# Every second weight block's low part made by an accumulating GpSimd transfer in a float32 decoder layer

## The chip, the core and the metric

The kernel runs on one core of one Trainium2 chip. The metric is the device time of one execution, in microseconds (us). The engines are named as the profile names them: PE is TensorE's matmuls and PEld its weight loads, DVE is VectorE, ACT is ScalarE, POOL is GpSimd and SP is SyncE, which here only issues loads. L92 is line 92 of the kernel's file. "q" behind an engine's name is its instruction queue.

## The reference

One decoder layer on 256 tokens of width 2048, all in float32: a gated feed-forward half, a mixer of two groups of attention heads, and a second feed-forward half, each behind an RMS norm.

```python
def swiglu(x, w_gate, w_up, w_down):
    return (jax.nn.silu(x @ w_gate) * (x @ w_up)) @ w_down

h = h + 0.5 * swiglu(rms_norm(h, norm_ffn1_g), ffn1_w_gate, ffn1_w_up, ffn1_w_down)
u = rms_norm(h, norm_mix_g)
q_f, k_f, v_f, f_logit, q_s, k_s, v_s = jnp.split(u @ w_in, SPLIT_POINTS, axis=-1)
...
o = jnp.concatenate([rms_norm(o_fox, out_norm_fox_g), rms_norm(o_swa, out_norm_swa_g)], axis=-1)
h = h + o @ w_out
h = h + 0.5 * swiglu(rms_norm(h, norm_ffn2_g), ffn2_w_gate, ffn2_w_up, ffn2_w_down)
```

The feed-forward width is 5632, so each of its three weights has 2048 x 5632 elements. The attention stands on 16 forgetting heads and 16 window heads (4 key-value heads) of width 64.

## The kernel before, in words

The weights are read once, in blocks of 128 partitions x 1024 float32 (512 KB). A matmul of type float32r takes operands with short mantissas, so each block is cut in two parts that add up to it: `whi`, the block rounded to float32r, and `wlo`, what the rounding left. The activations are cut in the same way. A product is then three products of parts: high by high, high by low, low by high.

`weights` (L89 to L95) does this for one block: SP issues the load into `raw` (L92), ScalarE makes `whi` by a rounding copy (L93), and VectorE makes `wlo` as `raw` minus `whi` (L94). The tiles come from `weight_tiles` (L83), which has four buffers each of `raw`, `whi` and `wlo`. A buffer is given to a later block when all readers of the earlier one are done: for `raw` these are L93 and L94, for `whi` and `wlo` the matmuls.

Two functions use the blocks. `columns` (L207) serves the feed-forward halves and the output projection: a block holds four row tiles of 128 x 256 weights, and `column_major` (L197) takes from it eight pairs of matmuls, L202 with `whi` against both parts of the activations (512 columns), L203 with `wlo` against their high part (256 columns). In a feed-forward half, `gate_up` (L243) loops over 22 chunks of 256 columns, four blocks of gate and four of up each; `gated` (L229) evacuates and combines them. `down` (L251) loops over 8 chunks of 11 blocks each. `token_major` (L277) serves the mixer's input projections, with two row tiles a block and the weights as the moving operand. In the output projection GpSimd multiplies (L681) and adds (L682) the evacuated tiles; it also adds up squares (L163).

The order of the instructions on each engine is set by the tile framework's scheduler from its own estimates of time; `weights` is called under a high priority, so loads, roundings and subtractions are placed as early as buffers allow. In the trace there are 648 roundings and as many subtractions: 600 of 128x1024, 32 of 128x776 (the window heads' projection) and 16 of 128x512, which are the first pieces of the first chunk. Those first pieces call `weights` with tiles of their own.

Of the kernel before, what the change touches and what calls it, by code (L numbers as in the profile page):

```python
# [17 lines left out]
P = 128  # L18
# [16 lines left out]

# columns of the constants and of the packed vectors
C_ID, C_ONE, C_TRI, C_MSK, C_INVF = 0, 128, 256, 384, 896
# [31 lines left out]
def hybrid_layer(ctx: ExitStack, tc: tile.TileContext, a: dict, out: bass.AP):  # L69
# [11 lines left out]

    # ---------------------------------------------------------------- weights
    def weight_tiles():  # L83
        raw = wp.tile([P, 1024], F32, tag="raw", name="raw", bufs=4)
        hi = wp.tile([P, 1024], F32R, tag="whi", name="whi", bufs=4)
        lo = wp.tile([P, 1024], F32R, tag="wlo", name="wlo", bufs=4)
        return raw, hi, lo

    def weights(src, tiles=None, at=0):  # L89
        """A block of weights: loaded, and cut into two parts of 12 bits that add up to it."""  # L90
        raw, hi, lo = (t[:, at : at + src.shape[1]] for t in tiles or weight_tiles())
        nc.sync.dma_start(raw, src)  # L92
        nc.scalar.copy(hi, raw)  # L93
        nc.vector.tensor_tensor(out=lo, in0=raw, in1=hi.bitcast(F32), op=ALU.subtract)  # L94
        return hi, lo  # L95

    # -------------------------------------------------------------- constants
    cst = keep.tile([P, C_END], F32, name="cst")
# [14 lines left out]
    def new_u():  # L113
        """The two parts of 2048 x 256 activations, by tiles of 128 rows."""
        halves = [half_u(0), half_u(1)]
        return lambda k: halves[k // 8][:, k % 8]
# [3 lines left out]

    # ----------------------------------------------------------- small helpers
    def mean_rsqrt(pool, ssq, n, width, tag):
        """1 / sqrt(ssq / width + EPS) for [P, n] sums, by Newton's steps."""
        x = pool.tile([P, n], F32, tag=tag + "x", name=tag + "x")
        y = pool.tile([P, n], F32, tag=tag + "y", name=tag + "y")
        t = pool.tile([P, n], F32, tag=tag + "t", name=tag + "t")
        nc.vector.tensor_scalar(
            out=x, in0=ssq, scalar1=1.0 / width, scalar2=EPS, op0=ALU.mult, op1=ALU.add
        )
        nc.vector.tensor_scalar(  # L130
            out=t.bitcast(I32), in0=x.bitcast(I32), scalar1=1, scalar2=None,
            op0=ALU.logical_shift_right,
        )
        nc.vector.tensor_scalar(
            out=y.bitcast(I32), in0=t.bitcast(I32), scalar1=-1.0, scalar2=float(0x5F3759DF),
            op0=ALU.mult, op1=ALU.add,
        )
        for _ in range(3):
            nc.vector.tensor_tensor(out=t, in0=y, in1=y, op=ALU.mult)
            nc.vector.scalar_tensor_tensor(  # L140
                out=t, in0=t, scalar=-0.5, in1=x, op0=ALU.mult, op1=ALU.mult
            )
            nc.vector.scalar_tensor_tensor(
                out=y, in0=t, scalar=1.5, in1=y, op0=ALU.add, op1=ALU.mult
            )
        return y

    def split_scaled(dst, src, gain):
        """dst = the two parts of src * gain, gain one value a partition."""
        nc.scalar.mul(dst[:, 0, :], src, gain)  # L150
        nc.vector.scalar_tensor_tensor(  # L151
            out=dst[:, 1, :], in0=src, scalar=gain, in1=dst[:, 0, :].bitcast(F32),
            op0=ALU.mult, op1=ALU.subtract,
        )

    def add_squares(ssq, src, first):
        """ssq [P, 2, SEQ] (+)= src squared."""
        if first:
            nc.scalar.activation(ssq, src, AF.Square)
            return  # L160
        sq = sp.tile([P, 2, SEQ], F32, tag="sqh", name="sqh", bufs=2)
        nc.scalar.activation(sq, src, AF.Square)  # L162
        nc.gpsimd.tensor_tensor(out=ssq, in0=ssq, in1=sq, op=ALU.add)  # L163

    def rstd_tokens(ssq, width, tag):
        """[P, NT], the tokens' 1 / rms, from sums of squares by partition."""
        pb = small_ps()
# [8 lines left out]
    def rstd_rows(ssq, width, tag):  # L176
        """[P, SEQ], the same in every partition."""
        r = rstd_tokens(ssq, width, tag + "t")
# [13 lines left out]

    # ------------------------------------------------------- feed-forward half
    def banks(acc):
        return acc[:, 0, :], acc[:, 1, :]

    def column_major(acc, w, u, k0, k, last, cols=(0, 1)):  # L197
        """acc[j] += (128 x 256 weights).T @ parts of u; its halves' sum is the product."""
        hi, lo = w
# [7 lines left out]
    def columns(acc, src, nk, u, apart=0):  # L207
        """acc = the products of nk row tiles; the columns' halves one after the other in the last ones."""
        late = []
# [57 lines left out]
    def into(u, ssq, gcol):  # L267
        """Of two row tiles of h that are finished: the parts for u, and the squares."""

# [7 lines left out]
    def token_major(acc, u, nk, src_w, width=512):  # L277
        """acc[:, t, :width] = u.T @ weights, for both token tiles."""
        for kg in range(nk // 2):
# [11 lines left out]

    # ------------------------------------------------------------ first FFN
    sp = ctx.enter_context(tc.tile_pool(name="sp", bufs=1))
    u1 = new_u()
    ss1 = sp.tile([P, 2, SEQ], F32, tag="ss", name="ss1")
    with tc.tile_pool(name="f1", bufs=1) as fp:
        hT = fp.tile([P, KF, 2, SEQ], F32R, name="hT1")
        # the tensor engine's clock rises while it works: products of zeros until the first operands come
        zero = fp.tile([P, 512], BF16, name="zero")
# [33 lines left out]

    # ------------------------------------------------------------ token mixer
    with tc.tile_pool(name="mix", bufs=1) as mp:
        ap_ = mp

        # angles of the rotation, reduced to [-pi, pi]
        n2 = NT * 32
# [62 lines left out]

        # ---- attention of four heads at a time
        def softmax_pv(scores, mask, vals, dst, nsk=None):
            """scores(j, blk, out): S of head j; vals(kb, j): values of key block kb; dst gets the heads' rows."""
            s0 = ap_.tile([P, 4, P], F32, tag="s0", name="s0", bufs=2)
# [36 lines left out]
            for i, s in ((0, s0), (1, s1_)):  # L443
                for j in range(4):
                    nc.vector.tensor_scalar_mul(s[:, j, :], s[:, j, :], rd[:, i, j : j + 1])
            # probabilities by key: of the first keys for all queries, of the second for the second
            p0 = ap_.tile([P, 4, SEQ], F32, tag="p0", name="p0", bufs=1)
# [15 lines left out]

        # ---- window heads and forget gates: columns f | q | k | v
        prs = ap_.tile([P, NT, NSW], F32, tag="prs", name="prs")
# [5 lines left out]

        # log of the forget gates, and its running sum
        z = ap_.tile([P, NT, NH], F32, name="z")
# [15 lines left out]

        # norms of the heads of q and k, and the rotation  # L490
        nqk = NH + NKV
# [16 lines left out]

        # of two k heads: the q heads, in pairs, and the k heads with zeros in the other half
        qk = [unit_tile([P, 6, SEQ], F32, "qk%d" % aa) for aa in range(2)]  # L510
        for aa in range(2):
            nc.gpsimd.memset(qk[aa][:, 4:6, :], 0.0)
        for t in range(NT):
# [3 lines left out]
            for j0, nj, tb in ((0, NH, tq), (NH, NKV, tk)):  # L517
# [3 lines left out]
                for es_, xa, ta, xb, tb_, op in (  # L521
# [7 lines left out]
                    nc.vector.tensor_tensor(out=o_, in0=o_, in1=w_, op=op)  # L529
            # q: pairs of heads of neighbouring k heads; k: each head with zeros in the other half  # L530
            rb_ = rw[:, t, :].unsqueeze(2).broadcast_to([P, nqk, HD])
# [37 lines left out]

        # ---- forgetting heads, by half: q and k carry the running sums  # L570
        ofx = ap_.tile([P, 8, SEQ], F32, name="ofx")
# [3 lines left out]
        def fox_qk(hf):  # L575
            aug[hf] = [unit_tile([HD + 2, 2, 4, SEQ], F32, "aug%d" % jj) for jj in range(2)]
            for i in range(2):
# [16 lines left out]
                for t in range(NT):  # L594
                    # columns 64 and 65: c and -1 for q; 1 and c for k
                    qa = ap_.tile([P, 8, HD + 2], F32, tag="qp", name="qa", bufs=2)
# [72 lines left out]

        # ---- output projection: window half, then forgetting half  # L670
        u2 = new_u()
# [13 lines left out]

    # ------------------------------------------------------------ second FFN
    rb2 = rstd_rows(ss2, D, "rb")
# [6 lines left out]

# ---- the arrays as the program reads them: blocks of weights as they are used, and vectors packed
def _arrays(x, positions, norm_ffn1_g, ffn1_w_gate, ffn1_w_up, ffn1_w_down, norm_mix_g, w_in, b_forget,
# [5 lines left out]
    def blocks(w, rows, cols):  # L702
        """By column block and group of row tiles, [P, tiles * columns] blocks."""
        n, m = w.shape
        w = w.reshape(n // P // rows, rows, P, m // cols, cols).transpose(3, 0, 2, 1, 4)
        return w.reshape(m // cols, n // P // rows, P, rows * cols)
# [57 lines left out]
```

## Time and profile before

| | |
|---|---|
| median of 2 runs | 1857.54 us (1857.29 to 1857.79) |
| the profiled execution's span, first to last instruction | 1855.6 us, 1.9 us below that median |
| TensorE, matmuls | 1842.8 us busy, 99% of the span |
| VectorE | 1142.0 us, 62% |
| ScalarE | 895.5 us, 48% |
| GpSimd | 91.1 us, 5% |
| DMA | 337.99 MB, 182 GB/s mean; the load queue holds the 16 engines 57.4% of the span |
| granted TensorE clock | 1.000 |

The profile is of one execution. Its own time is not listed apart from its span; what lies around the span is taken as the 1.9 us between the span and the median. Matmuls are pipelined and overlap, so a sum of their durations is more than the time that they take together. A row of a group of instructions has the line, the engine, the operation, what it writes and reads, the count, then the busy time and the mean of one in ns, and then the idle time of the engine before them with what ended it. A row of the list of waits reads: engine, tile and line that waited, what it waited for, us in total, times, the longest in us. A row of a timeline begins with start and duration in us. DMA issues give KB each and the us from issue to landing.

### The profile page before, as it was taken

To read this page: it belongs to the slowest core of one execution; us is meant where nothing else is said; L and a number is where in the kernel's file an instruction comes from. 1 tells how busy PE (TensorE), PEld (TensorE's weight loads), DVE (VectorE), ACT (ScalarE), POOL (GpSimd) and SP (SyncE) were. 2 spreads that over 40 slices of the span, in tenths; PEclk is the share of its full clock that TensorE was granted. 3 is DMA by queue.
4 is the path that set the end of the run, shared out by engine and by line. 5 is a ranking of instruction groups with operands and counts; after the bars stand their busy time and mean duration, and the time that the engine had idled before them with its cause. 6 is when DMAs were issued, how large, how long until landed. Compare 5 with 4: busy or idle time off the path is not lost.

```text
span 1855.6 us, 26310 instructions
## 1 busy us (share of the span) xinstructions
PE 1842.8 (99%) x10428; PEld 1604.5 (86%) x10428; DVE 1142.0 (62%) x1394; ACT 895.5 (48%) x1182; POOL 91.1 (5%) x73
## 2 busy tenths in 40 slices
PE   8999999999999999999999999999999999999999
PEld 6888888888888888998888888888888888888887
DVE  8556665655655555658767797566666666544443
ACT  6444444444444444455766655444444444443432
POOL 2000000000000000000001462000000000000000
PEclk9999999999999999999999999999999999999999
DMA  7666555665555565565345356666665655666663
GB/s 254 190 188 187 184 190 183 187 187 184 191 184 191 185 189 185 170 203 173 115 147 159 114 161 188 188 191 193 190 186 192 193 187 190 192 189 202 191 200 114
DMA packets 97211, 337.99 MB, mean 182 GB/s; under 512 B 10816, under 2 KB 12992, under 8 KB 97088
## 3 DMA queue, kind: packets, MB, share of 16 engines
q1 hardware_dynamic: 94752, 334.10, 57.4%
q10 hardware_dynamic: 2336, 2.21, 0.3%
q8 instruction: 82, 1.34, 0.3%
q14 instruction: 41, 0.34, 0.0%
HBM read 334.17 MB, written 2.10 MB: 181 GB/s over the span
## 4 chain that ended last, share of the span: by engine, by line
PE 97%; DVE 2%; issue 1%; ACT 1%; DMA 0%; DVEq 0%
PE acc L202 53%; PE acc L203 28%; PE acc L189 4%; PE acc L191 4%; PE acc L190 4%; DVE wlo L94 1%; PE sm L202 1%; PE sm L203 1%; PE sc L558 1%; PE sm L454 1%; PE sm L460 1%; PE sc L630 1%; DVE u L151 0%; PE sm L609 0%; PE sm L461 0%
## 5 line engine op out<-in xcount | busy, mean ns | idle before, releaser
L94 DVE TENSOR_TENSOR wlo<-raw,whi 128x1024 fp32r<-128x1024 f32 (+2 forms) x648 | 794.8, 1229 | 667.8 <-ACT whi L93 667.5
L93 ACT CAST whi<-raw 128x1024 fp32r<-128x1024 f32 (+2 forms) x648 | 665.7, 1029 | 897.0 <-PE acc L202 629.6
L202 PE MATMUL acc<-u,whi 128*128 128x512 f32 x2944 | 1033.2, 395 | 1.7 <-DVE t L226 1.0
L203 PE MATMUL acc<-u,wlo 128*128 128x256 f32 x2944 | 826.9, 281 | 4.2 <-DVE wlo L94 4.2
L202 PEld LDWEIGHTS acc<-u,whi 128*128 128x128 f32 x2944 | 551.9, 188 | 132.1 <-DVE t L226 1.3
L203 PEld LDWEIGHTS acc<-u,wlo 128*128 128x128 f32 x2944 | 556.2, 189 | 7.8 <-DVE wlo L94 7.0
L202 PE MATMUL acc<-hT,whi 128*128 128x512 f32 x1320 | 463.5, 393 | 0.0
L203 PE MATMUL acc<-hT,wlo 128*128 128x256 f32 x1320 | 373.3, 283 | 0.0
L202 PEld LDWEIGHTS acc<-hT,whi 128*128 128x128 f32 x1320 | 247.9, 188 | 57.3
L203 PEld LDWEIGHTS acc<-hT,wlo 128*128 128x128 f32 x1320 | 248.2, 188 | 0.0
L189 PE MATMUL acc<-whi,u 128*128 128x512 f32 (+1 forms) x320 | 120.1, 375 | 0.6 <-ACT pr L583 0.6
L191 PE MATMUL acc<-whi,u 128*128 128x512 f32 (+1 forms) x320 | 119.4, 373 | 0.0
L190 PE MATMUL acc<-wlo,u 128*128 128x512 f32 (+1 forms) x320 | 119.4, 373 | 0.0
L226 DVE TENSOR_TENSOR t<-acc,t 128x512 f32<-128x512 f32 x119 | 81.2, 682 | 0.0
L225 ACT COPY t<-acc 128x512 f32<-128x512 f32 x119 | 68.9, 579 | 0.7 <-PE acc L203 0.7
L189 PEld LDWEIGHTS acc<-whi,u 128*128 128x128 f32 x320 | 60.1, 188 | 8.6 <-ACT pr L583 0.8
L191 PEld LDWEIGHTS acc<-whi,u 128*128 128x128 f32 x320 | 60.1, 188 | 7.9 <-issue 0.6
L190 PEld LDWEIGHTS acc<-wlo,u 128*128 128x128 f32 x320 | 60.2, 188 | 7.1
L234 DVE TENSOR_TENSOR t<-t,rb 128x512 f32<-128x512 f32 x88 | 60.7, 692 | 2.9
L202 PE MATMUL acc<-oTf,whi 128*128 128x512 f32 x128 | 45.4, 396 | 1.0 <-DVE t L226 1.0
L163 POOL TENSOR_TENSOR ssm<-ssm,sqh 128x512 f32<-128x512 f32 x7 | 9.6, 1367 | 704.8 <-ACT sqh L162 704.8
L151 DVE SCALAR_TENSOR_TENSOR u<-h,vec,u 128x256 fp32r<-128x256 f32 x48 | 40.1, 875 | 3.7 <-ACT u L150 3.7
(185 smaller groups left out, 812.6 us busy)
## 6 DMA issues: line engine op xcount, KB each, us to landing
raw<-in_wd SPq DMA_DIRECT2D x176, 512.0 KB, 3.5
raw<-in_wg SPq DMA_DIRECT2D x172, 512.0 KB, 3.5
raw<-in_wu SPq DMA_DIRECT2D x172, 512.0 KB, 3.5
raw<-in_wf SPq DMA_DIRECT2D x48, 512.0 KB, 3.9
raw<-in_wo SPq DMA_DIRECT2D x32, 512.0 KB, 3.6
raw<-in_ws SPq DMA_DIRECT2D x32, 388.0 KB, 3.1
h<-in_xT SPq DMA_DIRECT2D x8, 256.0 KB, 5.1
raw<-in_wg SPq DMA_DIRECT2D x8, 256.0 KB, 4.4
```

The lines of the kernel that those rows point to most:

```text
L93: nc.scalar.copy(hi, raw)
L94: nc.vector.tensor_tensor(out=lo, in0=raw, in1=hi.bitcast(F32), op=ALU.subtract)
L151: nc.vector.scalar_tensor_tensor(out=dst[:, 1, :], in0=src, scalar=gain, in1=dst[:, 0, :].bitcast(F32), op0=ALU.mult, op1=ALU.subtract,)
L189: nc.tensor.matmul(o, lhsT=shi, rhs=mhi, start=start, stop=False)
L190: nc.tensor.matmul(o, lhsT=shi, rhs=mlo, start=False, stop=False)
L191: nc.tensor.matmul(o, lhsT=slo, rhs=mhi, start=False, stop=stop)
L202: nc.tensor.matmul(acc[j], lhsT=hi[:, s], rhs=u(k), start=(k == 0), stop=False)
L203: nc.tensor.matmul(acc[j][:, 0:SEQ], lhsT=lo[:, s], rhs=u(k)[:, 0, :], start=False, stop=(k == last - 1))
L225: nc.scalar.copy(t, acc[:, :, SEQ:])
L226: nc.vector.tensor_tensor(out=t, in0=acc[:, :, 0:SEQ], in1=t, op=ALU.add)
L234: nc.vector.tensor_tensor(out=v[nm], in0=v[nm], in1=rbb, op=ALU.mult)
L454: nc.tensor.transpose(bt[:, j * P : (j + 1) * P], src[:, j, :], ident)
```

## The change

Of the blocks that get their own tiles, the second, fourth and so on make `wlo` in another way. ScalarE writes minus `raw`, rounded to float32r, into `wlo`; then GpSimd issues a transfer from `raw` to `wlo` that adds to what is there. The sum is again `raw` minus its rounded part. `raw` has three buffers where it had four, and `wlo` five where it had four. The other blocks, and the first chunk's pieces, are made as before. Below, "odd" blocks are those with the subtraction and "even" ones those with the transfer.

```diff
     def weight_tiles():
-        raw = wp.tile([P, 1024], F32, tag="raw", name="raw", bufs=4)
+        raw = wp.tile([P, 1024], F32, tag="raw", name="raw", bufs=3)
         hi = wp.tile([P, 1024], F32R, tag="whi", name="whi", bufs=4)
-        lo = wp.tile([P, 1024], F32R, tag="wlo", name="wlo", bufs=4)
+        lo = wp.tile([P, 1024], F32R, tag="wlo", name="wlo", bufs=5)
         return raw, hi, lo

+    turn = [0]
+
     def weights(src, tiles=None, at=0):
         raw, hi, lo = (t[:, at : at + src.shape[1]] for t in tiles or weight_tiles())
         nc.sync.dma_start(raw, src)
         nc.scalar.copy(hi, raw)
-        nc.vector.tensor_tensor(out=lo, in0=raw, in1=hi.bitcast(F32), op=ALU.subtract)
+        turn[0] += tiles is None
+        if tiles is None and turn[0] % 2 == 0:
+            nc.scalar.mul(lo, raw, -1.0)
+            nc.gpsimd.dma_start(lo, raw, accum_op=ALU.add)
+        else:
+            nc.vector.tensor_tensor(out=lo, in0=raw, in1=hi.bitcast(F32), op=ALU.subtract)
         return hi, lo
```

Comments are gone too, and lines behind `weights` stand eight lower: L95 is now the load, L96 the rounding, L99 the negation, L100 the transfer, L102 the subtraction, L210 and L211 the matmuls, L689 and L690 GpSimd's multiply and add. In the rows below a number behind a tile's name counts tiles in the order of the program, and the names in brackets are the semaphores waited for: those of engines, DMAHW for loads, DMASW for GpSimd's transfers.

SP, loads of the gate and up weights of the first feed-forward half. Before, every load waits for VectorE alone, besides the earlier load into the same buffer:

```order
L92 DMA raw_969<-in_wg1 128x1024 [waits DMAHW7_49,DVE_49]
L92 DMA raw_991<-in_wg1 128x1024 [waits DMAHW0_49,DVE_49]
L92 DMA raw_1013<-in_wg1 128x1024 [waits DMAHW1_49,DVE_49]
L92 DMA raw_1035<-in_wg1 128x1024 [waits DMAHW2_49,DVE_49]
L92 DMA raw_1058<-in_wu1 128x1024 [waits DMAHW3_49,DVE_49]
```

The same place now. The four blocks of a group are 1175 (odd), 1197 (even), 1220 (odd), 1242 (even):

```order
L95 DMA raw_1117<-in_wu1 128x1024 [waits DMAHW6_49,DMASW5_49,Activation_49]
L95 DMA raw_1139<-in_wu1 128x1024 [waits DMAHW7_49,DVE_49]
L95 DMA raw_1175<-in_wg1 128x1024 [waits DMAHW1_49,DVE_49]
L95 DMA raw_1197<-in_wg1 128x1024 [waits DMAHW0_49,DMASW6_49]
L95 DMA raw_1220<-in_wg1 128x1024 [waits DMAHW2_49,DMASW7_49,Activation_49]
L95 DMA raw_1242<-in_wg1 128x1024 [waits DMAHW3_49,DVE_49]
L95 DMA raw_1266<-in_wu1 128x1024 [waits DMAHW5_49,DVE_49]
L95 DMA raw_1288<-in_wu1 128x1024 [waits DMAHW4_49,DMASW0_49]
```

The second and the third load of each group of four now wait for a transfer of GpSimd: raw_1197 for that of block 1094, four blocks back, and raw_1220 for that of block 1139, three blocks back. The first and the fourth wait for subtractions, two and three blocks back. In the down weights' part the same list alternates: an odd block waits for the subtraction two blocks back, an even one for the transfer four blocks back.

ScalarE at the same blocks, now:

```order
L96 CAST whi_1176<-raw_1175 128x1024 [waits DMAHW3_49,DVE_49,PE_49]
L243 ACTIVATE t_1162<-t_1162 128x512 [waits DVE_49]
L96 CAST whi_1198<-raw_1197 128x1024 [waits DMAHW4_49,PE_49,Activation_49]
L99 ACTIVATE wlo_1199<-raw_1197 128x1024 [waits DMASW3_49]
L96 CAST whi_1221<-raw_1220 128x1024 [waits DMAHW5_49,PE_49,Activation_49]
L99 ACTIVATE wlo_1244<-raw_1242 128x1024 [waits DMAHW6_49,DMASW4_49,PE_49]
L96 CAST whi_1243<-raw_1242 128x1024 [waits PE_49,Activation_49]
L233 COPY t_1166<-acc_1071 128x512 [waits PE_49]
```

The four roundings stand as before, with two negations between them; that of the fourth block stands ahead of its rounding.

GpSimd in the output projection, now (before, only the rows of `t` and `h` and some others stood there, with no transfer between):

```order
L100 DMA wlo_9296<-raw_9294 128x1024 [waits DMASW5_49,DMAHW0_49,DVE_49,Activation_49]
L609 MEMSET qa_8707 128x8 [waits PE_49]
L689 TENSOR_TENSOR t_9215<-t_9215,rs_8101 128x512 [waits DVE_49]
L609 MEMSET qa_8723 128x8 [waits PE_49,Pool_49]
L690 TENSOR_TENSOR h_67<-h_67,t_9215 128x512 [waits Pool_49]
L100 DMA wlo_9347<-raw_9345 128x1024 [waits DMAHW2_49,DMASW6_49,Activation_49]
L689 TENSOR_TENSOR t_9266<-t_9266,rs_8101 128x512 [waits DVE_49]
L690 TENSOR_TENSOR h_67<-h_67,t_9266 128x512 [waits Pool_49]
L100 DMA wlo_9398<-raw_9396 128x1024 [waits DMAHW4_49,DMASW7_49,Activation_49]
```

A transfer stands behind the multiply and the add of an earlier tile there. In the feed-forward halves GpSimd's queue holds hardly anything but transfers: all in all 316, of which 16 are 128x776.

## The prediction

> **What bounds the kernel now.** I read the page's first part, then the chain that ended last, then the list of who waited for whom.
>
> ```profile
> span 1855.6 us, 26310 instructions
> PE 1842.8 (99%) x10428; PEld 1604.5 (86%) x10428; DVE 1142.0 (62%) x1394; ACT 895.5 (48%) x1182; POOL 91.1 (5%) x73
> PE 97%; DVE 2%; issue 1%; ACT 1%; DMA 0%; DVEq 0%
> ```
>
> TensorE is busy for all but 12.8 us of the span (1855.6 - 1842.8), and 97% of the chain is TensorE. VectorE, which the change relieves, has 2% of the chain. The list of waits says the same of the place itself:
>
> ```profile
> DVE wlo L94 <- ACT whi L93: 667.5, 564, 4.4
> ACT whi L93 <- PE acc L202: 629.6, 381, 2.2
> POOL t L681 <- DVE t L226: 45.5, 14, 7.0
> PEld acc L203 <- DVE wlo L94: 7.0, 8, 1.8
> PE acc L203 <- DVE wlo L94: 4.2, 6, 1.5
> ACT whi L93 <- DMA raw<-in_wu: 3.7, 1, 3.7
> ```
>
> Columns are us in total, times, longest. VectorE waits for ScalarE's rounding, and ScalarE waits for TensorE to give a `whi` buffer back. TensorE itself waits for a low part in 6 cases, for 4.2 us in all; ScalarE waited for a load of `raw` from `in_wu` once. Everything ahead of TensorE therefore runs early and is held back by buffers. **A faster way to make low parts cannot win more than a few us.** What the change can do is use up the lead. So the question is how much lead there is, and how long the new path takes.
>
> **The pace to be kept.** Inside the first feed-forward half, the timeline of ScalarE and VectorE:
>
> ```profile
> 205.35 1.05 ACT L93 CAST whi<-raw 128x1024 fp32r<-128x1024 f32 x1 [1.78 <-PE acc L202]
> 206.43 1.23 DVE L94 TENSOR_TENSOR wlo<-raw,whi 128x1024 fp32r<-128x1024 f32 x1 [1.61 <-ACT whi L93]
> 208.17 1.05 ACT L93 CAST whi<-raw 128x1024 fp32r<-128x1024 f32 x1 [1.29 <-issue]
> 216.65 1.05 ACT L93 CAST whi<-raw 128x1024 fp32r<-128x1024 f32 x1 [1.77 <-PE acc L202]
> ```
>
> From 205.35 to 216.65 lie four blocks: 11.3 us, so **2.82 us a block**, and that is TensorE's pace. A rounding takes 1.05 us, a subtraction 1.23 us.
>
> **The change part by part.** It takes 316 subtractions (300 of 128x1024, 16 of 128x776) off VectorE, some 316 x 1.23 = 390 us of an engine that is busy 62%. VectorE is not what TensorE waits for, so this is worth 0, and at most the 11.2 us of the two rows above.
>
> It adds 316 negations on ScalarE, as wide as the rounding: 316 x 1.05 = 330 us, so ScalarE goes from 48% to about 66%. Over four blocks it then has 6 x 1.05 us and two evacuating steps of about 0.6 us, 7.5 of 11.3 us. By its sum this is hidden in the 629.6 us that ScalarE now waits for TensorE; what counts is that the negation stands in a chain with the transfer.
>
> It adds 316 accumulating transfers of 512 KB. The trace has none, so I bound one from the weight loads, which are as large:
>
> ```profile
> raw<-in_wd SPq DMA_DIRECT2D x176, 512.0 KB, 3.5
> raw<-in_wg SPq DMA_DIRECT2D x172, 512.0 KB, 3.5
> raw<-in_wu SPq DMA_DIRECT2D x172, 512.0 KB, 3.5
> ...
> q1 hardware_dynamic: 20437, 74.45, 59.3%
> L92 SPq DMA_DIRECT2D raw<-in_wu x52: 327/328/328, 210.5 to 490.3; - x52
> L163 POOL TENSOR_TENSOR ssm<-ssm,sqh 128x512 f32<-128x512 f32 x7 | 9.6, 1367 | 704.8 <-ACT sqh L162 704.8
> L94 DVE TENSOR_TENSOR wlo<-raw,whi 128x1024 fp32r<-128x1024 f32 x142 | 174.0, 1225 | 166.5 <-ACT whi L93 166.5
> ```
>
> A load lands 3.5 us after its issue. The fourth row is the load queue between 200 and 600 us of the span: 59.3% of the 16 engines' time. The last row counts 142 blocks in those 400 us, so one load holds all engines for 0.593 x 400 / 142 = **1.67 us**. An accumulating transfer must read `raw`, read the old `wlo` and write `wlo`, where a load has one read and one write. Low end: as cheap as a load, 1.67 us of engines; high end: three passes, 5.0 us. I take 2.5 us, one half more than the load that is its nearest row. GpSimd must first prepare the transfer: at least the 0.33 us of SP's issue, at most the 1.37 us of its own 128x512 addition; I take the middle, 0.85 us. From the end of the negation to the landing, **D** = 0.85 + 3.5 + (2.5 - 1.67) = 5.2 us with nothing in the way. A load runs 59% of the time, on the same engines; I add one load's 1.67 us, so D = 6.9 us. Low end 0.33 + 3.5 = 3.8, high end 1.37 + 3.5 + 3.33 + 1.67 = 9.9.
>
> [...]
>
> It moves the release of `raw`. SP's own list of waits shows what gates a load now:
>
> ```profile
> SPq L92 <- DVE wlo L94: 1469.7, 600, 7.9
> ```
>
> Every load waits for a subtraction four blocks back, at four buffers. With three, the rows of the order above give two kinds of loop that no buffer cuts short:
>
> - Gate and up blocks: the third load of a group of four waits for the accumulating transfer of the fourth block before it. One turn over four blocks is load, rounding, negation, D. Bare: 3.5 + 1.05 + 1.05 + 5.2 = 10.8 us, under the 11.3 us available. But load and accumulation now meet. With 1.67 us on D, and half an accumulation, 1.25 us, ahead of the load: 10.8 + 1.67 + 1.25 = 13.7 us, **3.43 us a block, +0.61 us**.
> - Down blocks: odd blocks own one `raw` buffer, so load, rounding and subtraction must turn within two blocks: 3.5 + 1.05 + 1.23 = 5.78 us, against 5.65 us. That is +0.07 us a block with nothing in the way. With a quarter of an accumulation, 0.63 us, on the load: 6.41 / 2 = 3.2 us, +0.38 us a block.
>
> The engines' sum alone over four blocks is 4 x 1.67 + 2 x 2.5 = 11.7 us, +0.1 us a block, so at 2.5 us the loops decide and not the bandwidth.
>
> The mixer, with 112 blocks in windows of less transfer:
>
> ```profile
> 815.00:980.00 165.00, 164.44 (x847) 137.30 (x846) 123.57 (x257) 100.75 (x200) 4.94 (x9) 1.00 0.48 153
> 980.00:1110.00 130.00, 128.96 (x766) 109.56 (x765) 104.70 (x149) 83.53 (x151) 52.17 (x37) 1.00 0.46 146
> ```
>
> (length; busy us of PE, PEld, DVE, ACT, POOL with counts; granted clock; DMA share; GB/s). The share is 0.46 to 0.48, as attention stands between the runs of blocks, so I take half of the gate blocks' price, 0.3 us a block. In the output projection the transfers stand behind GpSimd's multiply (L681) and add (L682) of `t` and `h`; the former waits for VectorE (45.5 us in 14 cases above), and the transfer waits with it. That is inside the 0.3.
>
> Sum: gate and up 344 x 0.61 = 210; down 176 x 0.38 = 67; mixer 112 x 0.3 = 34. Together **+311 us** on the span of 1855.6 us. The median of the runs is 1857.5 us, 1.9 us above that span, so 1855.6 + 311 + 1.9 = about **2168 us**.
>
> **Rivals.**
>
> *The lead suffices* (ends on the other side: not slower). The accumulating transfer costs no more than a load, and is hidden: D = 3.8 us, the gate loop is 3.5 + 2.1 + 3.8 = 9.4 us, and only the down blocks' 0.07 x 176 = 12 us are lost, less at most 11 us of waits for low parts gained: 1857 to 1870 us. For it: the engines' share of 0.59 leaves room for 2 x 1.67 us in 11.3. Against it: the second read, and a lead that ends at 11.3 - 5.6 = 5.7 us for D in the gate blocks. It decides from there: below 5.7 us nothing is lost.
>
> *Several whole passes.* At 3.34 us (two reads one after the other) the engines' sum is 13.4 us; the gate loop 3.5 + 2.1 + 0.85 + 3.5 + 1.67 + 1.67 + 1.67 = 15.0 us, 3.74 a block, +0.92; down 5.78 + 1.67 = 7.45 us, +0.9 a block; with half of it in the mixer: 316 + 158 + 50, about 2380 us. At 5.0 us the engines are the bound, (6.7 + 10) / 4 = 4.17 us a block, +1.35: 1.35 x 520 + 0.7 x 112 = 780, about 2640 us.
>
> *GpSimd held off by VectorE.* GpSimd's 128x512 additions of `ssq` spread over a range:
>
> ```profile
> L163 POOL TENSOR_TENSOR ss<-ss,sqh x14: 1284/1470/1836, 7.1 to 1126.3; 128x512 f32<-128x512 f32 x14
> ```
>
> 1.28 to 1.84 us for one shape: something holds it at times. If a remaining subtraction held the preparing of a transfer for its whole 1.23 us, D would be 8.1 us and the gate loop 14.9 us, 3.73 a block: 344 x 0.91 + 67 + 112 x 0.45 = 430, about 2290 us. [...]
>
> That the change is not what it says can be left out: the order shows 316 transfers on GpSimd and 316 subtractions fewer.
>
> **How the numbers follow.** The forecast's case (loops of buffers at 2.2 to 3 us of engines, 1900 to 2300 us) 0.50; lead suffices 0.13; several passes 0.27; held off 0.10. The range goes from the first rival's upper end, 1870, to 2600, below the dearest case; it leaves out about 0.1 at each end. About 2% is what a measurement of this kernel can tell from no change. Faster by over 2% would need 37 us where the waits are 12.8 us: 0.02. Within 2% (to 1895 us) is the first rival: 0.11. Slower: 0.87.
>
> **What would show it.** TensorE's busy time falls behind the span, in gaps before matmuls of `wlo` (L211 now) released by DMA; SP waits for DMA rather than for VectorE; ScalarE's roundings wait for loads; the DMA share goes to 0.85 or more; VectorE falls by about 390 us, ScalarE rises by about 330 us. A gap before `whi` rather than `wlo` speaks for loads that come late. The loss per block should be larger in gate and up than in down, and smallest in attention. I am wrong if D is below 5.7 us beside loads, which ends near 1865 us, or if the engines carry an accumulation at far below a load's rate, which passes 2600 us.

## The result and the profile after

The change makes the kernel slower: **2214.52 us** (median of 2 runs, 2208.61 to 2220.43) against 1857.54 us, ratio 1.194 (95% interval 1.1834 to 1.2046). That is 357 us more; the forecast was 311 us more, 2168 us. The first part of the page after, its DMA queues, its chain, and its DMA issues:

```profile
span 2218.3 us, 27122 instructions
PE 1950.4 (88%) x10428; PEld 1650.3 (74%) x10428; DVE 768.5 (35%) x1078; ACT 1187.6 (54%) x1498; POOL 358.3 (16%) x389
...
q1 hardware_dynamic: 94752, 334.10, 45.0%
q0 software_dynamic: 45504, 163.66, 40.1%
...
DMA 74%; issue 11%; ACT 5%; PE 4%; DVE 4%; SPq 1%; POOLq 0%; POOL 0%; ACTq 0%; DVEq 0%
...
L100 POOL DMA_DIRECT2D wlo<-raw x316 | 272.9, 864 | 1787.6 <-ACT wlo L99 1315.7
...
wlo<-raw POOLq DMA_DIRECT2D x300, 512.0 KB, 6.1
raw<-in_wd SPq DMA_DIRECT2D x176, 512.0 KB, 4.4
```

The row of L100 is GpSimd's own step, which prepares a transfer (864 ns); the last column of the last two rows is the time to the landing, counted from the start of the step that issues the transfer. Before, TensorE was 97% of the chain; now transfers are 74% of it, and TensorE stands still for 267.9 us of the span (2218.3 - 1950.4). Its 10428 matmuls also take 107.6 us longer (1950.4 - 1842.8), of which the last section tells. VectorE has lost 373.5 us and ScalarE has gained 292 us. Queue q0 carries the new transfers: 40.1% of 2218.3 us over 316 of them is 2.81 us of the 16 engines each, beside 45.0% over some 637 blocks' worth of loads (334.10 MB), 1.57 us each. Loads now land 4.4 us after their issue, where it was 3.5 us.

What TensorE and ScalarE wait for, and then what SP's queue waits for (us in total, times, longest):

```profile
PEld acc L211 <- DMA wlo<-raw: 260.2, 159, 4.6
...
ACT whi L96 <- DMA raw<-in_wu: 240.8, 114, 4.9
...
PE acc L211 <- DMA wlo<-raw: 210.0, 138, 4.2
...
ACT whi L96 <- PE acc L210: 31.3, 19, 3.5
```

```profile
SPq L95 <- DMA wlo<-raw: 937.2, 297, 8.2
```

Each wait of before has turned round. ScalarE's rounding waited 629.6 us for TensorE to give a `whi` buffer back; now that is 31.3 us, and it waits for loads instead. A load waits for an accumulating transfer in 297 cases. Of TensorE's waits, those for the low part of a transferred block lead the list. Hardly anything runs ahead any longer.

The chain between 300 and 330 us of the span, in the gate and up blocks (start, length, what):

```profile
304.53 4.81 DMA raw<-in_wg
...
309.41 1.38 issue
...
310.79 7.19 DMA wlo<-raw
...
318.79 5.46 DMA raw<-in_wu
...
325.71 6.86 DMA wlo<-raw
```

This is one closed turn over four blocks: a transfer lands, SP issues a load, the load lands, ScalarE negates (1.06 of the 1.38 us named "issue"), GpSimd issues the next transfer, which frees the next load. Of the two loads that SP issues there one behind the other, the chain goes through the second. From 310.79 to 325.71 it took 14.9 us; the turn before it, 13.9 us.

Where the 362.7 us of span went is read from SP's loads, by the time of the first load of each phase. Before (the first two rows count the loads up to 1200 us of the span, the others those from 1000 us on):

```profile
L92 SPq DMA_DIRECT2D raw<-in_wd x88: 327/328/328, 493.1 to 737.7; - x88
...
L92 SPq DMA_DIRECT2D raw<-in_ws x32: 327/328/328, 740.5 to 811.6; - x32
...
L92 SPq DMA_DIRECT2D raw<-in_wg x88: 327/328/328, 1096.0 to 1573.2; - x88
...
L92 SPq DMA_DIRECT2D raw<-in_wd x88: 327/328/328, 1587.1 to 1831.2; - x88
```

After (the same):

```profile
L95 SPq DMA_DIRECT2D raw<-in_wd x88: 327/328/502, 595.8 to 875.8; - x88
...
L95 SPq DMA_DIRECT2D raw<-in_ws x32: 327/328/391, 879.4 to 971.2; - x32
...
L95 SPq DMA_DIRECT2D raw<-in_wg x88: 327/328/1602, 1297.5 to 1887.6; - x88
...
L95 SPq DMA_DIRECT2D raw<-in_wd x88: 327/328/1034, 1905.9 to 2197.3; - x88
```

| phase (from its first load to the next phase's) | blocks | before, us | after, us | lost, us | a block |
|---|---|---|---|---|---|
| start, gate and up of the first half | 168 and the first pieces | 493.1 | 595.8 | 102.7 | 0.61 |
| down, first half | 88 | 247.4 | 283.6 | 36.2 | 0.41 |
| mixer | 112 | 355.5 | 418.1 | 62.6 | 0.56 |
| gate and up, second half | 176 | 491.1 | 608.4 | 117.3 | 0.67 |
| down, second half, to the end | 88 | 268.5 | 312.4 | 43.9 | 0.50 |

The first row holds the start too: the first load of a whole block stands at 23.6 us before and at 26.3 us after, so some 3 us were lost ahead of the blocks. Without them gate and up lost 217 us, down 80 us, the mixer 62.6 us. The first eight whole blocks alone lost 13 of the 217 us (the load behind them starts at 40.4 us before, at 56.5 us after).

### The profile page after: what moved, and what is told of

It is laid out like the page before. It is cut to its first block, busy times and chain, and to the rows that moved or that the text cites. A ratio compares the mean times of both kernels' runs of the same rounds, so it can differ in the third digit from the quotient of the medians.

```text
span 2218.3 us, 27122 instructions
## 1 busy us (share of the span) xinstructions
PE 1950.4 (88%) x10428; PEld 1650.3 (74%) x10428; DVE 768.5 (35%) x1078; ACT 1187.6 (54%) x1498; POOL 358.3 (16%) x389
## 3 DMA queue, kind: packets, MB, share of 16 engines
q1 hardware_dynamic: 94752, 334.10, 45.0%
q0 software_dynamic: 45504, 163.66, 40.1%
## 4 chain that ended last, share of the span: by engine, by line
DMA 74%; issue 11%; ACT 5%; PE 4%; DVE 4%; SPq 1%; POOLq 0%; POOL 0%; ACTq 0%; DVEq 0%
DMA wlo<-raw 35%; DMA raw<-in_wd 12%; DMA raw<-in_wu 12%; DMA raw<-in_wg 9%; ACT whi L96 3%; DMA raw<-in_wf 2%; DVE wlo L102 2%; DMA raw<-in_wo 2%; DMA raw<-in_ws 1%; PE acc L210 1%; SPq L95 1%; ACT s L440 1%; PE acc L211 1%; ACT wlo L99 0%; PE sc L638 0%
## 5 line engine op out<-in xcount | busy, mean ns | idle before, releaser
L96 ACT CAST whi<-raw 128x1024 fp32r<-128x1024 f32 (+2 forms) x648 | 660.5, 1022 | 776.4 <-DMA raw<-in_wu 240.8
L210 PE MATMUL acc<-u,whi 128*128 128x512 f32 x2944 | 1074.9, 406 | 0.4 <-DVE u L159 0.2
L211 PE MATMUL acc<-u,wlo 128*128 128x256 f32 x2944 | 855.8, 291 | 152.0 <-DMA wlo<-raw 146.0
L102 DVE TENSOR_TENSOR wlo<-raw,whi 128x1024 fp32r<-128x1024 f32 (+2 forms) x332 | 400.7, 1209 | 1159.9 <-ACT whi L96 1159.9
L211 PEld LDWEIGHTS acc<-u,wlo 128*128 128x128 f32 x2944 | 574.8, 195 | 188.1 <-DMA wlo<-raw 178.7
L210 PEld LDWEIGHTS acc<-u,whi 128*128 128x128 f32 x2944 | 571.6, 194 | 132.7 <-ACT whi L96 1.3
L100 POOL DMA_DIRECT2D wlo<-raw x316 | 272.9, 864 | 1787.6 <-ACT wlo L99 1315.7
L210 PE MATMUL acc<-hT,whi 128*128 128x512 f32 x1320 | 472.5, 398 | 0.0
L99 ACT ACTIVATE wlo<-raw 128x1024 fp32r<-128x1024 f32 (+1 forms) x316 | 330.9, 1047 | 223.8 <-DMA raw<-in_wd 120.6
L211 PE MATMUL acc<-hT,wlo 128*128 128x256 f32 x1320 | 380.8, 289 | 60.3 <-DMA wlo<-raw 59.8
L211 PEld LDWEIGHTS acc<-hT,wlo 128*128 128x128 f32 x1320 | 252.0, 191 | 77.2 <-DMA wlo<-raw 75.8
L210 PEld LDWEIGHTS acc<-hT,whi 128*128 128x128 f32 x1320 | 251.2, 191 | 55.8
L198 PE MATMUL acc<-wlo,u 128*128 128x512 f32 (+1 forms) x320 | 125.0, 391 | 32.3 <-DMA wlo<-raw 31.3
L210 PE MATMUL acc<-oTf,whi 128*128 128x512 f32 x128 | 47.2, 407 | 3.6 <-DVE t L234 3.6
```

The lines of the kernel that those rows point to most:

```text
L99: nc.scalar.mul(lo, raw, -1.0)
L100: nc.gpsimd.dma_start(lo, raw, accum_op=ALU.add)
L198: nc.tensor.matmul(o, lhsT=shi, rhs=mlo, start=False, stop=False)
L210: nc.tensor.matmul(acc[j], lhsT=hi[:, s], rhs=u(k), start=(k == 0), stop=False)
L211: nc.tensor.matmul(acc[j][:, 0:SEQ], lhsT=lo[:, s], rhs=u(k)[:, 0, :], start=False, stop=(k == last - 1))
```

## Experiments

The theory after this result was the forecast's: three buffers of `raw`, and a transfer in the loop that gives them back (called "Loop" in the expectations). The rivals were that the 16 DMA engines are simply full ("Engines"), and that the low part comes too late for TensorE whatever the buffers are ("Late"). Below, buffer counts are given as `raw`/`whi`/`wlo`: the kernel before has 4/4/4, the changed one 3/4/5. Every ratio is against the kernel before.

| run | blocks with a transfer | what | buffers | us | ratio (95%) |
|---|---|---|---|---|---|
| changed kernel | every 2nd | accumulating | 3/4/5 | 2214.52 | 1.194 (1.1834 to 1.2046) |
| e1_raw4 | every 2nd | accumulating | 4/4/4 | 2009.21 | 1.0833 (1.072 to 1.0947) |
| e5_hbm | every 2nd | accumulating, from HBM | 3/4/5 | 2024.97 | 1.0918 (1.0829 to 1.1007) |
| e3_plain | every 2nd | plain copy | 3/4/5 | 2170.14 | 1.1701 (1.1622 to 1.1779) |
| e14_raw4_plain | every 2nd | plain copy | 4/4/4 | 1914.46 | 1.0322 (1.025 to 1.0394) |
| e6_every4 | every 4th | accumulating | 3/4/5 | 2115.6 | 1.1422 (1.1333 to 1.1512) |
| e13_raw4_every4 | every 4th | accumulating | 4/4/4 | 1874.14 | 1.0105 (1.0035 to 1.0174) |
| e11_raw5 | every 2nd | accumulating | 5/3/4 | 2163.34 | 1.1663 (1.1536 to 1.1791) |
| e12_raw5_every4 | every 4th | accumulating | 5/3/4 | 1998.5 | 1.0775 (1.0705 to 1.0844) |
| e4_vadd | none | VectorE adds | 3/4/5 | 1864.88 | 1.0039 (0.9996 to 1.0083) |
| e7_side | every 2nd, beside the work | one scratch tile | 3/4/4 | 2116.1 | 1.141 (1.1334 to 1.1485) |
| e9_side2 | every 2nd, beside the work | two scratch tiles | 3/3/4 | 1922.82 | 1.0382 (1.0283 to 1.048) |
| e10_control | none | as before | 3/3/4 | 1862.9 | 1.0054 (1.0013 to 1.0094) |

### The transfer alone, without the buffers' change: e1_raw4

```diff
-        raw = wp.tile([P, 1024], F32, tag="raw", name="raw", bufs=3)
+        raw = wp.tile([P, 1024], F32, tag="raw", name="raw", bufs=4)
...
-        lo = wp.tile([P, 1024], F32R, tag="wlo", name="wlo", bufs=5)
+        lo = wp.tile([P, 1024], F32R, tag="wlo", name="wlo", bufs=4)
```

> The change with raw back at four buffers and wlo at four (the same memory). Three theories. Loop: what is lost is the turn load, negation, accumulation, next load of a raw buffer, 14.9 us over four blocks with three buffers; a fourth buffer lengthens the turn's allowance by a third (to about 15 us at TensorE's pace), so most comes back: 1870 to 1980 us. Engines: the 16 DMA engines are too full, buffers don't matter: 2180 to 2250 us. Late part: negation and accumulation, some 8 us, don't fit into the lead that the whi and wlo buffers leave: 2150 to 2250 us, or more with the wlo buffer less.

2009.21 us: 205 of the 357 us come back, with the same memory and the same transfers, and 152 us stay. So none of the three theories is right by itself: the time lies above the range of Loop and below those of the others. The first feed-forward half in stretches (length; busy us of PE, PEld, DVE, ACT, POOL; granted clock; DMA share; GB/s), and three waits:

```profile
60.00:520.00 460.00, 436.48 (x2438) 373.48 (x2437) 166.92 (x190) 268.48 (x304) 65.55 (x76) 1.00 0.98 261
```

```profile
ACT whi L96 <- PE acc L210: 452.0, 258, 5.1
...
PEld acc L211 <- DMA wlo<-raw: 133.4, 111, 3.2
PE acc L211 <- DMA wlo<-raw: 97.8, 84, 2.9
```

The engines are held 98% of the time, where the changed kernel has 88% in its first half (the same view):

```profile
60.00:580.00 520.00, 459.95 (x2467) 389.97 (x2466) 171.57 (x191) 273.45 (x308) 65.53 (x76) 0.97 0.88 233
```

With the fourth buffer ScalarE is again ahead and waits for TensorE (452.0 us). What is left goes with full engines and with TensorE's waits for transfers (97.8 us before its matmuls); this run does not tell the two apart. With three buffers, the engines have 12% to spare and the turn decides.

### No transfer at all, everything else of the change: e4_vadd

```diff
-            nc.gpsimd.dma_start(lo, raw, accum_op=ALU.add)
+            nc.vector.tensor_tensor(out=lo, in0=raw, in1=lo.bitcast(F32), op=ALU.add)
```

> The change's buffers (3, 4, 5) and its negation on ScalarE, but VectorE adds raw to the negated part where GpSimd's transfer did. No transfer is left of the change. If the transfer is the whole cause (turn of buffers and engines both), 1855 to 1875 us. If three raw buffers or 330 us more of ScalarE cost by themselves, 1900 us or above.

1864.88 us, ratio 1.0039. The negation is there, and so are the three buffers of `raw`:

```profile
PE 1834.7 (99%) x10428; PEld 1604.4 (87%) x10428; DVE 1129.7 (61%) x1394; ACT 1195.7 (65%) x1498; POOL 92.1 (5%) x73
```

ScalarE at 1195.7 us and three buffers cost 7 us at most, which the interval does not tell from nothing. The rest of the loss belongs to the transfer.

### A plain copy in place of the accumulation: e3_plain and e14_raw4_plain

```diff
-            nc.gpsimd.dma_start(lo, raw, accum_op=ALU.add)
+            nc.gpsimd.dma_start(lo, raw)
```

The sum is left out, so `wlo` gets `raw` itself. In e14_raw4_plain the buffers are 4/4/4 besides.

> The change with a plain transfer from raw to wlo in place of the accumulating one (the low part of every second block is then wrong: the sum is left out). It reads one stream where the accumulation reads two. If the accumulation's own price (2.9 us of engines against 1.5 to 1.7 for a load) matters, the landing comes 1.2 us sooner, and less is in the way of loads. Loop: turn 14.9 - 1.2 - 0.6 = 13.1 us, 3.3 us a block, 1980 to 2080 us. Engines: 4 x 1.6 + 2 x 1.6 = 9.6 us of 11.3, so 1860 to 1930 us. Late part: 1950 to 2100 us.

2170.14 us, a miss: only 44 us come back. Queue q0 and the landing of the plain copy:

```profile
q0 software_dynamic: 45504, 163.66, 20.7%
...
wlo<-raw POOLq DMA_DIRECT2D x300, 512.0 KB, 6.1
```

The copy holds the engines half as long (20.7% of 2166.8 us over 316 is 1.42 us, against 2.81 us), yet it lands no sooner: 6.1 us, as the accumulation does. I had expected the landing to fall with the engine time. The turn is made of landing times, so it stayed.

> Buffers of four each, every second block, with a plain transfer from raw to wlo in place of the accumulating one (the sum is left out, so low parts of every second block are wrong). A plain transfer needs half the engines' time (20.7% against 40.1% of the span, at three raw buffers) and landed no sooner there (6.1 us). If full engines are the rest of the 152 us, 1870 to 1920 us; if the landing's latency is, 1960 to 2010 us.

```profile
q0 software_dynamic: 45504, 163.66, 24.2%
...
wlo<-raw POOLq DMA_DIRECT2D x300, 512.0 KB, 5.0
```

1914.46 us: at four buffers the same halving of engine time brings 95 of the 152 us back, inside the range for full engines. But the copy also lands sooner here than the accumulation does (5.0 us against 6.3 us in e1_raw4), so fuller engines and later landings are not told apart. At three buffers the landing did not move, and little came back.

### Half as many transfers: e6_every4 and e13_raw4_every4

```diff
-        if tiles is None and turn[0] % 2 == 0:
+        if tiles is None and turn[0] % 4 == 0:
```

> The change for every fourth block instead of every second; buffers 3, 4, 5. The engines then need 4 x 1.57 + 2.81 = 9.1 us of 11.3. Engines: nothing lost, 1858 to 1890 us. Turn of buffers: one accumulation in four blocks; three buffers hold together one block of about 13 us and three of about 6.5 us in 11.3 us, 32.5 / 3 = 10.8 us of 11.3, so little is lost: 1860 to 1930 us. A loss in proportion to the transfers (178 us, 2035 us) would speak for a price of each transfer that no slack hides.

2115.6 us: with half the transfers, 258 of the 357 us are still lost. The expectation counted buffers, and missed. Its chain between 300 and 330 us, and the stretch from 300 to 500 us:

```profile
301.61 6.13 DMA wlo<-raw
...
308.54 4.95 DMA raw<-in_wu
...
314.95 6.25 DMA wlo<-raw
...
327.44 6.34 DMA wlo<-raw
```

```profile
300.00:500.00 200.00, 182.00 (x1005) 155.51 (x1004) 89.27 (x96) 96.82 (x112) 13.80 (x16) 0.98 0.70 204
```

The engines are held 70% of the time and TensorE still waits. From transfer to transfer it is 13.3 and 12.5 us for four blocks, above the 11.3 us of the pace. SP's queue shows how one transfer in four closes a turn; these are its loads in program order, with what each waits for:

```
L95 DMA raw_1131<-in_wu1 128x1024 [waits DMAHW7_49,DVE_49]
L95 DMA raw_1167<-in_wg1 128x1024 [waits DMAHW0_49,DVE_49]
L95 DMA raw_1189<-in_wg1 128x1024 [waits DMAHW1_49,DVE_49]
L95 DMA raw_1211<-in_wg1 128x1024 [waits DMAHW2_49,DMASW7_49,Activation_49]
L95 DMA raw_1233<-in_wg1 128x1024 [waits DMAHW3_49,DVE_49]
```

Block 1131 has a transfer, and block 1233 has the next. The buffer of 1131 is taken by 1211, whose load waits for that transfer. Block 1233 takes the buffer of 1167, which a subtraction gives back; but its load stands right behind the waiting one in SP's queue and went out behind it: in the stretch of the chain above SP issued no load from 301.64 to 308.10 us, and then two within 0.80 us. So the next transferred block can't even be loaded until the last transfer has landed. Of those two loads, the one that the turn needs is the second.

> Buffers of four each, as in the experiment that lost 152 us, but every fourth block accumulated instead of every second. There the engines were 0.95 to 0.98 busy in the feed-forward halves; here they need 9.1 of 11.3 us. If full engines were the rest of that loss, 1858 to 1890 us. If it was the turn through TensorE's release of whi (rounding, negation, 0.3 us, accumulation 6.2 to 6.9 us: 8.6 to 9.3 us in the 8.5 us of three blocks), half as many transfers lose up to half: 1880 to 1940 us. As much as 1998 us (5, 3, 4 buffers) would mean that four buffers help no more than three of whi.

```profile
300.00:500.00 200.00, 199.01 (x1133) 172.80 (x1133) 97.47 (x106) 107.20 (x124) 14.62 (x17) 1.00 0.80 234
```

1874.14 us: the fourth buffer takes the loss at every fourth block from 258 to 17 us. That is inside the range given for full engines, and below the one for the turn through `whi`. In the same stretch TensorE is busy for 199.0 of 200 us at an engine share of 0.80. The pair speaks most clearly for the turn: the same transfers, the same memory, engines short of full in both, 241 us apart. The semaphores in the two traces show why. In e6_every4 each of the 157 loads that wait for a transfer stands three blocks behind the transferred one, so the next transferred block, four behind, is held up. In e13_raw4_every4, 130 of 156 such loads stand five blocks behind: the next transferred block is loaded ahead of them, and the turn spans eight blocks.

### Contention alone: e7_side, e9_side2 and e10_control

Here VectorE makes all low parts, as before, and 316 accumulating transfers run beside the work, into scratch tiles that nobody reads; e10_control has e9_side2's buffers and no transfers.

```diff
+    sides = [wp.tile([P, 1024], F32R, tag="side%d" % i, name="side%d" % i, bufs=1) for i in range(2)]
...
+        if tiles is None and turn[0] % 2 == 0:
+            nc.gpsimd.dma_start(sides[turn[0] // 2 % 2][:, : src.shape[1]], lo.bitcast(F32), accum_op=ALU.add)
```

> The kernel before with three raw buffers, four of wlo, all low parts by VectorE, and beside it 316 accumulating transfers of the low part of every second block into a scratch tile that nobody reads. The engines carry the same accumulations, nobody waits for them but the wlo buffer. Loop: 1858 to 1900 us. Engines: 2100 to 2250 us. Late part: 1858 to 1900 us.

With one scratch tile: 2116.1 us. That it lies in the range of Engines tells nothing, because I had built a new chain. Each transfer waits for the one before it into the same tile, and `wlo` waits with it:

```profile
POOL side L101 <- DMA side<-wlo: 1555.4, 286, 7.2
```

> As the experiment with a scratch tile, but with two scratch tiles in turn, so that the scratch accumulations don't wait for one another (one tile made them a chain of 6.6 us each); buffers 3 of raw, 3 of whi, 4 of wlo. 316 accumulations beside a kernel that does not wait for them. Engines: 4 x 1.57 + 2 x 2.81 = 11.9 us over four blocks where TensorE needs 11.3, so 2.97 us a block, 1930 to 2010 us. Turn of buffers alone: 1858 to 1880 us, if its own control shows no loss.

> The control of the experiment with two scratch tiles: the kernel before with 3 buffers of raw, 3 of whi and 4 of wlo, and no transfers of GpSimd. All theories: 1855 to 1875 us, as a block's load, rounding and subtraction (5.8 us) fit in three blocks (8.5 us).

With two scratch tiles: 1922.82 us, against 1862.9 us of the control; it lies between the ranges of the two theories.

```profile
300.00:500.00 200.00, 195.68 (x1100) 167.67 (x1099) 114.58 (x119) 88.19 (x103) 29.46 (x35) 1.00 1.00 270
```

The engines are full here (share 1.00), and even so 316 transfers that only the `wlo` buffers wait for cost 60 us (1922.82 - 1862.9). I take that as the price of sharing the engines, with three buffers of `raw`. If prices add, it leaves some 300 of the change's 357 us, and some 90 of the 152 us of e1_raw4, to what waits for a transfer's landing.

### A fifth buffer of raw, paid by whi: e11_raw5 and e12_raw5_every4

```diff
-        raw = wp.tile([P, 1024], F32, tag="raw", name="raw", bufs=3)
-        hi = wp.tile([P, 1024], F32R, tag="whi", name="whi", bufs=4)
-        lo = wp.tile([P, 1024], F32R, tag="wlo", name="wlo", bufs=5)
+        raw = wp.tile([P, 1024], F32, tag="raw", name="raw", bufs=5)
+        hi = wp.tile([P, 1024], F32R, tag="whi", name="whi", bufs=3)
+        lo = wp.tile([P, 1024], F32R, tag="wlo", name="wlo", bufs=4)
```

> The change with buffers 5 of raw, 3 of whi, 4 of wlo in place of 3, 4, 5 (the same memory). A raw buffer held by an accumulation is then asked for again five blocks later, so the turn accumulation, load, negation, accumulation spans six blocks (16.9 us at TensorE's pace) and takes some 14 us. If the turn is the main loss, what is left is the engines' share as seen with two scratch tiles (65 us) and a few late low parts: 1920 to 1990 us. If the accumulations themselves come too late for TensorE, 2050 to 2200 us, with waits for wlo as in the change.

> As the one before with every fourth block instead of every second: the turn spans eight blocks, the engines need 9.1 of 11.3 us. If turn and engines are all there is, 1858 to 1890 us, against 2116 us for every fourth block with buffers 3, 4, 5. If an accumulation is dear by itself, some 1950 us or more.

2163.34 us and 1998.5 us. Both are far above what turn and engines alone would give; they lie in the ranges for accumulations that come too late for TensorE (2050 to 2200 us) and for one that is dear by itself (1950 us or more). The waits of e11_raw5:

```profile
ACT whi L96 <- PE acc L210: 632.1, 421, 8.6
PEld acc L211 <- DMA wlo<-raw: 234.7, 133, 4.8
```

The loads are early now, but rounding and negation stand in one queue on ScalarE. With three buffers of `whi` a rounding waits for TensorE to finish the block three back, the negation behind it waits along, and the transfer's landing is too late for TensorE. TensorE waits for the transfer (234.7 us in its weight loads) although ScalarE waits for TensorE (632.1 us): the lead of the low part is too short. So the theory called Late holds with three buffers of `whi`: against e1_raw4 there is one buffer more of `raw` and one less of `whi`, and the kernel loses 154 us by it (2163.34 - 2009.21). In e10_control the same three buffers of `whi` cost 5 us; there a subtraction of 1.2 us follows the rounding, and not a negation and 6 us of transfer. The lead comes from `raw` and from `whi` both, and a transfer uses all of it.

### The accumulation fed from HBM: e5_hbm

```diff
-            nc.gpsimd.dma_start(lo, raw, accum_op=ALU.add)
+            nc.gpsimd.dma_start(lo, src, accum_op=ALU.add)
```

The transfer reads the weights a second time, so it no longer holds `raw`, and the turn is cut at three buffers.

> The change with the accumulating transfer reading the weights from HBM once more in place of raw; buffers 3, 4, 5 as in the change. raw is then free after the negation, so the turn has no accumulation in it. Loop: 1860 to 1980 us, SP waits no more for the accumulations. Engines: as much or more to carry, 2200 us or above. Late part: 2100 to 2250 us, TensorE waits for wlo as now.

2024.97 us, above the range of Loop and below the others: 190 us are back, nearly as much as with the fourth buffer (205 us). The transfer itself is no cheaper:

```profile
q0 software_dynamic: 45504, 163.66, 45.3%
...
wlo<-in_wd POOLq DMA_DIRECT2D x88, 512.0 KB, 8.6
```

It lands after 8.6 us instead of 6.1 and holds the engines 2.91 us (45.3% of 2027.4 us over 316). So the hold on `raw` cost at least these 190 us, although the transfer got longer. The 167 us that stay were not taken apart. No version with transfers beat the kernel before; the nearest is e13_raw4_every4 at 1.0105.

## Why the prediction was right, and where its terms were off

The forecast of slower by the loops of buffers held: 357 us measured, 311 us predicted, and all but 7 us of it is the transfer's (e4_vadd). Taken by its steps:

- **A faster way to low parts wins nothing: right.** VectorE fell by 373.5 us (390 predicted) with no gain, and ScalarE's added 292 us (330 predicted) cost 7 us at most where no transfer stands behind them (e4_vadd).
- **The gate and up loop: right in kind and size.** Predicted 13.7 us per four blocks, 3.43 a block; measured 608.4 / 176 = 3.46 a block in the second half. 210 us were predicted, 217 were lost. But I had built the turn from the third load, its rounding and the negation. In the trace the rounding isn't in it (the fourth block's negation stands ahead of its rounding); instead there are the two issues on SP and the wait of one load behind another (0.81 us from the transfer's landing to the next load in the chain above, 0.47 us in the turn before it). That 1.05 us too much and these too little nearly cancel is luck. e6_every4 missed because I still counted buffers and not SP's order.
- **D, from the negation's end to the landing: near.** 6.9 us predicted; measured 6.1 us to the landing and some 0.3 us between the negation and GpSimd's step, 6.4 us. GpSimd's preparing, 0.85 us as the middle of two rows of other work, is 0.864 us, which is luck; it is part of the 6.1 us. In the same way the 3.5 us of a load already held the 0.33 us of SP's step, so the forecast's sum put GpSimd's step on top of SP's. A transfer's engine time, 2.5 us predicted, is 2.81 us. Its landing spreads from 4.3 to 10.0 us (a load's from 2.6 to 9.7 us):

```profile
L100 POOL DMA_DIRECT2D wlo<-raw x316: 852/862/1010, 34.1 to 2205.3; - x158
...
DMA to landing us min/median/max: 4.3/6.0/10.0
```

- **The down blocks: the size near, the reason open.** 67 us predicted, 80 lost. I had made it the odd blocks' loop of load, rounding and subtraction in two blocks. The chain shows the even blocks' turn instead (here at 650 to 680 us):

```profile
662.28 7.58 DMA wlo<-raw
669.88 4.34 DMA raw<-in_wd
...
675.67 6.87 DMA wlo<-raw
```

  13.4 us for four blocks. Yet SP waits more for VectorE than for transfers in this part (86.2 us and 42.9 us between 620 and 860 us of the span, and 81.6 us for the landing of a load), as the odd blocks' loop would have it. The two were not told apart by a run.
- **The mixer: under-sized by half.** "half of the gate blocks' price, 0.3 us a block" was 0.56: 62.6 us instead of 34. It rested on a DMA share of 0.46 to 0.48, and the share doesn't set a turn; e6_every4 at 0.70 shows that. Nor is the loss smallest there: 0.56 a block against 0.41 and 0.50 in down. By the two profiled executions the loss is 362.7 us, 52 us above the sum: this term is 29 of them, down 13, gate and up 7, and the 3 us ahead of the first whole block had no term.
- **The lead suffices: fell.** It needed D below 5.7 us; D was 6.4 us. Its 3.8 us were SP's 0.33 us of issue and a load's 3.5 us; in these runs an accumulating transfer of 512 KB landed after 4.7 us at the least median (every fourth block, four buffers; e13_raw4_every4), and a plain copy after 5.0 us (four buffers, e14_raw4_plain) and 6.1 us (three, e3_plain). Where the landing was shortest, at 4.7 us, D was some 5.0 us and little was lost (e13_raw4_every4), as this rival's rule has it, though with half as many transfers and a longer turn.
- **Several whole passes: half of it is there.** 2.81 us are 1.8 loads' engine time, between the 2.5 us of the forecast and the 3.34 us of this rival. With three buffers it mattered little (44 us for halving it, e3_plain); with four, halving it and landing 1.3 us sooner brought back 95 of 152 us (e14_raw4_plain).
- **GpSimd held off by VectorE: fell.** Preparing took 852 to 1010 ns, median 862; a hold for a whole subtraction of 1.23 us would show as rows of 2 us. In the changed kernel only 18 of the 316 preparations ran beside a subtraction, but in e7_side 296 did, and there too they took 852 to 1010 ns, median 862. So no such hold shows in either run.
- **What would show it.** Gaps before `wlo` matmuls ended by transfers, SP waiting for DMA, roundings waiting for loads, a share of 0.88: all seen. I had read a share of 0.85 and more as a sign of the forecast, and it is as high with the turn cut (0.98, e1_raw4); the share alone tells nothing.

## What to carry to other kernels

When a transfer becomes the last reader of a buffer, price the whole closed turn (landing, the next issue, the next load, the engine's step, landing again; 14.9 us here) against the pace that the consumers need (11.3 us here), and not the transfer's share of the engines. Read the turn from the order of the issuing queue, and not from the count of buffers alone: in e6_every4 a load that waited held back the loads behind it, and one slow release in four blocks cost 258 us where a fourth buffer of the same kind left 17 (e13_raw4_every4). A buffer moved from one tile to another at equal memory can be worth far more (205 us here) than halving the work that seems to be in the way (44 us).

## What the runs showed of the hardware that I had not expected

TensorE's granted clock was lower behind waits of TensorE. Over the whole span it is 0.969, where it was 1.000 before. As an estimate, that is worth 69 us of full-speed time (0.031 x 2218.3), and it added no more than those 69 us to the 107.6 us by which the matmuls took longer. Three stretches of 3.4 us of the changed kernel, one after the other (columns as before, the clock third from the end):

```profile
348.20:351.60 3.40, 3.40 (x20) 2.78 (x19) 0.04 (x1) 1.52 (x2) 0.86 (x1) 1.00 0.79 233
351.60:355.00 3.40, 0.99 (x6) 0.83 (x6) 1.89 (x3) 2.48 (x3) 0.86 (x1) 0.99 0.76 140
355.00:358.40 3.40, 3.40 (x13) 2.92 (x12) 1.16 (x2) 1.56 (x2) 0.00 (x0) 0.51 1.04 252
```

After a stretch in which TensorE worked for 0.99 of 3.4 us, the next one runs at 0.51 and takes 13 matmuls, where 20 were taken at 1.00. The span has 37 such pieces at half the clock, 136.5 us in all; in the 3.4 us ahead of each, TensorE had worked for 1.65 us at most. Ahead of the piece shown here it was idle for 71% of the stretch, with 2.41 us as the longest gap. How much of the loss is due to these pieces stays open: while the turn decides, a slower TensorE may hide in its waits, and no run took the drop away by itself. They are rarer where TensorE waits less (clock 0.993 in e1_raw4, 0.997 in e13_raw4_every4), but the sum of the waits does not set them: e3_plain has 0.989 with TensorE idle for 245.8 us, in more and shorter waits (197 of 2.7 us at most before L211's matmuls, against 138 of 4.2 us at most). So the 44 us of e3_plain may be a matter of the clock as well; that is not shown.

The other surprise is the plain copy from GpSimd: half the engine time of the accumulation (1.42 against 2.81 us), and the same 6.1 us to its landing beside the loads at three buffers. What sets that landing, if not the engines' time, the runs don't tell.
